# A decoder trunk whose instruction order is planned: 32 plans with wider margins, one of them emitted

## The chip, the cores and the metric

The kernel runs on one core of a Trainium2 chip. A core has five engines that work side by side, each through its own list of instructions in order: TensorE (PE, matrix products; its weight loads are shown apart as PEld), VectorE (DVE), ScalarE (ACT), GpSimd (POOL) and SyncE (SP, which here only issues transfers, DMAs). An engine whose next instruction has to wait holds up all that stands behind it in its list. The metric is the device time of one execution in microseconds (us); lower is better.

## The reference

Two layers of a sequence model over 2048 tokens of width 1024, all in float32. Layer 0 mixes tokens by a gated delta rule (GDN, 8 heads), layer 1 by gated linear attention (GLA, 4 heads). Each has an input projection, a recurrence over chunks of the sequence, a gated RMS norm, an output projection and a layer norm.

```python
def gdn_mixer(x, w_in, conv_w, a_log, dt_bias, norm_w, w_out):
    p = x @ w_in
    qkv = causal_conv_silu(p[..., :GDN_QKV], conv_w)
    ...
    o = gated_delta_rule(q, k, v, g, beta)
    o = gated_rmsnorm(o, norm_w, gate)
    return o.reshape(B, T, GDN_VAL).astype(x.dtype) @ w_out
...
for i in range(DEPTH):
    ...
    x = layer_norm(DEEP_ALPHA * x + y, ln_g[i], ln_b[i])
```

## The kernel before

The work is cut into 48 units: a layer, a group of 512 tokens and a head, in the order of `PHASES` (L1189: GDN groups 0 and 1, GLA group 0, GDN 2, GLA 1, GDN 3, GLA 2, GLA 3). A GDN unit has four parts. `gemms` (L650) multiplies the group's tokens by the head's columns of the input matrix: for each 128 rows of it a chunk `wc` holds a rounded high part and a remainder in two halves, and three 512-column products (high by high, high by low, low by high: `xh,wc`, `xl,wc`, `xh,wc`) go into a `psg` bank of PSUM. `gdn_prep` (L800) builds a triangular matrix and inverts it: 32-wide blocks by a loop of 31 steps on VectorE (`Xt` and `X`, L861 to L866) that reads rows spread to all partitions by eight DMAs (`Arep`, L855), then larger blocks on TensorE with ScalarE copying between the products (`U` to `W2` to `U`, L870 to L885). `gdn_chain` (L1020) runs the recurrence, with a ScalarE copy `wt` between two of its products. `outs` (L1095) multiplies by the output matrix into the one bank of `pso`, six products at a time, and VectorE adds each bank into `y` (L1119) before the next six may start.

Chunks of the input matrix come from memory as `wraw` and are split by ScalarE and GpSimd in the first units (L529); from the third unit on the split chunk is written back (`wk`, L531), and each later group reads it from there straight into `wc` (L516). `wc` has 9 buffers (L1180), so a reload can start only when TensorE has read the chunk that was in the buffer. All these loads, the spread rows `Arep`, the stores `out` and the loads of `y` stand in one list on SP.

No engine's order is written by hand. The unit functions only record operations (`Recorder.note`, L133), with their dependences, a rank (L1185: recurrence before preparation before output before projection), and an estimated time: `cost`, how long the engine is held, and `lag`, how much later the result can be used (L183 to L232). `place` (L234) is a list scheduler: it keeps a clock for each engine, always takes the engine that can go first, gives it the ready operation of the best rank, hands out the buffers as they come free, and so fixes the order. `emit` (L357) then issues the operations in that order, and the hardware's engines go through their lists with real waits. The whole program is issued through one line, L364, so the profile's rows are told apart by the tiles' names.

Of the kernel before, what the change touches and what calls it, by code (L numbers as in the profile page):

```python
# [107 lines left out]

class Op:
    __slots__ = ("key", "call", "name", "args", "kw", "prio", "cost", "lag", "deps", "users", "waits", "ready",  # L110
                 "views", "fresh", "start", "at", "func", "unit")


def size_of(shape):
# [6 lines left out]
class Recorder:  # L121
# [226 lines left out]
    def stuck(self, parked, free, order_of, turn):  # L348
        for tag, ops in parked.items():
# [4 lines left out]
            nxt = {k[1]: ts[turn[k]].at if turn[k] < len(ts) and ts[turn[k]] else None for k, ts in order_of.items() if k[0] == tag}  # L354
            print("   live", live, "next", nxt)

    def emit(self, tc):  # L357
        if INSPECT:
            INSPECT(self)
        def real(a):  # L360
            return a.real() if isinstance(a, View) else a

        for op in self.place():
            tc.keep_in_program_order(op.call(*[real(a) for a in op.args], **{k: real(a) for k, a in op.kw.items()}))  # L364


# [11 lines left out]
LAG, DRAIN = 60, 35  # L378
DMA_LAG, REP_LAG, SLACK = 3500, 7000, 100
INSPECT = None  # L380


@with_exitstack
# [846 lines left out]
```

## Time and profile before

| what | value |
|---|---|
| median of 3 runs | 3030.2 us (3029.43 to 3033.52) |
| the profiled execution, its own time | 3028.51 us |
| its span, first to last instruction | 3026.3 us |
| mean granted TensorE clock over the span | 0.988 |
| TensorE busy / VectorE busy | 2926.2 us / 2201.4 us |
| HBM read and written | 480.36 MB, 129.30 MB |

The profile is a record of one execution. A row of the list of waits names the engine that waited, what it waited for, the sum in us, how often, and the longest. A row of the windows view gives, for a stretch of the span, each engine's busy time, then the granted TensorE clock (1.00 is full speed), the DMA engines' busy share and GB/s. A row of the timeline gives start, length, engine, line, operation, tiles written and read, and in brackets the engine's idle time before it and what ended that. A matmul's shown length holds its passage through the array, and the next starts before it ends, so the distance from start to start is what one costs. A 4-byte product (`f32` on both sides) goes as two instructions.

### The profile page before, as it was taken

How to read it: one execution, taken by the hardware profiler on the slowest of the kernel's cores; microseconds unless marked ns; L12 is line 12 of the kernel's file. 1: busy time of each engine (PE TensorE's matmuls, PEld its weight loads, DVE VectorE, ACT ScalarE, POOL GpSimd, SP SyncE). 2: the span in 40 equal slices, each digit the busy share in tenths (PEclk: the TensorE clock that was granted, in tenths of full speed). 3: DMA queues.
4: the chain of work that ended last, by engine and by line, in shares of the span. 5: the costliest groups of instructions: out<-in, count | busy, mean ns of one | idle time of the engine just before them, and what ended most of it. 6: DMA issues, size and time to landing. Idle time of an engine off the chain costs nothing. (4 is left out here: it accounts for less than half of the span.)

```text
span 3026.3 us, 48052 instructions
## 1 busy us (share of the span) xinstructions
PE 2926.2 (97%) x16172; PEld 2419.0 (80%) x16172; DVE 2201.4 (73%) x5374; ACT 1243.6 (41%) x3233; POOL 499.8 (17%) x848
## 2 busy tenths in 40 slices
PE   8899999999999999999999999999999999999997
PEld 6677777778877887887888888887787888888886
DVE  6878788797777686668778778557787777755655
ACT  5445554543332455333343344333343344433331
POOL 5432444320100233210000000001010000000000
PEclk9999999999999999999999999999999999999998
DMA  6566777695565658687556665768655565857654
GB/s 193 175 196 203 239 234 241 209 293 159 167 182 178 191 165 269 213 286 224 161 163 182 190 207 179 242 228 244 175 171 176 154 193 176 268 192 236 221 183 143
DMA packets 480615, 612.87 MB, mean 203 GB/s; under 512 B 57280, under 2 KB 407744, under 8 KB 464240
## 3 DMA queue, kind: packets, MB, share of 16 engines
q1 hardware_dynamic: 449456, 589.81, 62.9%
q10 hardware_dynamic: 30912, 20.00, 2.4%
q8 instruction: 127, 2.08, 0.3%
q14 instruction: 120, 0.98, 0.1%
HBM read 480.36 MB, written 129.30 MB: 201 GB/s over the span
## 5 line engine op out<-in xcount | busy, mean ns | idle before, releaser
L364 PE MATMUL psg<-xh,wc 128*128 128x512 f32 x3936 | 1349.5, 409 | 29.0 <-DMA wc<-wk 16.3
L364 PEld LDWEIGHTS psg<-xh,wc 128*128 128x128 f32 x3936 | 740.5, 190 | 195.8 <-DMA wc<-wk 20.6
L364 PE MATMUL psg<-xl,wc 128*128 128x512 f32 x1968 | 805.8, 410 | 0.2
L364 PE MATMUL pso<-wo,oth 128*128 128x512 f32 x1472 | 486.1, 406 | 19.1 <-DVE y L364 17.6
L364 PEld LDWEIGHTS psg<-xl,wc 128*128 128x128 f32 x1968 | 374.4, 190 | 76.4 <-DVE xl L364 1.7
L364 DVE SCALAR_TENSOR_TENSOR y<-pso,z,y 128x512 f32<-128x512 f32 x368 | 274.9, 747 | 148.6 <-PE pso L364 127.6
L364 DVE SCALAR_TENSOR_TENSOR acc<-pb,taps,acc 128x512 f32<-128x512 f32 x384 | 300.3, 785 | 76.5 <-ACT acc L364 69.2
L364 POOL TENSOR_TENSOR wc<-wraw,wc 128x256 fp32r<-128x256 f32 (+1 forms) x336 | 283.3, 859 | 423.5 <-ACT wc L364 360.3
L364 PEld LDWEIGHTS pso<-wo,oth 128*128 128x128 f32 x1472 | 263.9, 189 | 82.8 <-DVE y L364 29.0
L364 PE MATMUL pso<-wo,otl 128*128 128x512 f32 x736 | 295.8, 402 | 0.6 <-DVE otl L364 0.6
L364 PE MATMUL psg<-wc,xh 128*128 128x256 f32 (+1 forms) x1344 | 265.3, 289 | 6.2 <-DMA wc<-wk 4.6
L364 DVE TENSOR_TENSOR Xt<-Arep,X 128x124 f32<-128x124 f32 (+30 forms) x992 | 238.6, 241 | 30.6 <-DMA Arep<-blk 7.5
L364 DVE TENSOR_TENSOR X<-X,Xt 128x124 f32<-128x124 f32 (+30 forms) x992 | 242.6, 245 | 23.9
L364 ACT ACTIVATE th<-psg 128x512 f32<-128x512 f32 (+1 forms) x170 | 95.2, 572 | 334.4 <-PE psg L364 315.4
L364 PEld LDWEIGHTS psg<-wc,xh 128*128 128x128 f32 x1344 | 214.6, 189 | 15.0 <-DMA wc<-wk 4.6
L364 PE MATMUL psg<-wc,xl 128*128 128x256 f32 (+1 forms) x672 | 189.4, 287 | 0.0
L364 ACT CAST wc<-wraw 128x256 fp32r<-128x256 f32 (+1 forms) x336 | 126.0, 405 | 116.2 <-DMA wraw<-in_w_in 99.3
L364 PEld LDWEIGHTS pso<-wo,otl 128*128 128x128 f32 x736 | 139.1, 189 | 30.6 <-DVE otl L364 1.6
L364 POOL TENSOR_SCALAR z<-ssq 128x4 f32<-128x4 f32 x44 | 16.8, 383 | 804.7 <-ACT junk L364 804.2
L364 ACT COPY pb<-psg 128x512 f32<-128x512 f32 x128 | 74.8, 585 | 148.4 <-PE psg L364 145.6
L364 POOL COPY halo<-pb 128x3 f32<-128x3 f32 x128 | 35.2, 275 | 577.6 <-ACT pb L364 576.3
L364 PEld LDWEIGHTS psg<-wc,xl 128*128 128x128 f32 x672 | 126.1, 189 | 2.7
(193 smaller groups left out, 4280.3 us busy)
## 6 DMA issues: line engine op xcount, KB each, us to landing
wc<-wk SPq DMA_DIRECT2D x856, 256.0 KB, 3.8
wo<-wok SPq DMA_DIRECT2D x70, 1024.0 KB, 5.0
wk<-wc SPq DMA_DIRECT2D x272, 256.0 KB, 3.0
wraw<-in_w_in SPq DMA_DIRECT2D x336, 128.0 KB, 3.5
Arep<-blk SPq DMA_DIRECT2D x128, 256.0 KB, 5.4
wok<-wo SPq DMA_DIRECT2D x24, 1024.0 KB, 5.3
wc<-wk SPq DMA_DIRECT2D x80, 272.0 KB, 5.3
Arep<-blkq SPq DMA_DIRECT2D x128, 128.0 KB, 6.4
```

What stands on the lines that cost most here:

```text
L364: tc.keep_in_program_order(op.call(*[real(a) for a in op.args], **{k: real(a) for k, a in op.kw.items()}))
```

## The change

`place` is now called by a new function `choose`, 32 times. Each time the costs of all operations are set anew: 20 ns more for each VectorE operation, 300 ns more until a ScalarE result can be used, a transfer's time to landing times 1.3, and every cost times a drawn factor between 0.98 and 1.02. The order that comes out is then carried out by a second model, `carry_out`: engines in order, the plain costs, landing times from a table by tile (`LANDINGS`) times a drawn factor, at most eight transfers under way, and VectorE operations that are now and then 450 ns longer while GpSimd is at work. Four draws are averaged, and the order with the earliest mean end is emitted. The operations, their number, the tiles and the buffers stay the same; the order on every engine changes, and with it which buffer a tile gets.

```diff
+    def choose(self):
+        import random
+        true = [(op.cost, op.lag) for op in self.ops]
+        for op in self.ops:
+            op.real = self.landing(op)
+        best = None
+        for n in range(N_PLANS):
+            draw = random.Random(n)
+            for op, (cost, lag) in zip(self.ops, true):
+                more, times, late = MARGIN.get(op.key, (0, 1.0, 0))
+                op.cost, op.lag = (cost + more) * draw.uniform(0.98, 1.02), lag * times + late
+                op.waits, op.ready = len(op.deps), 0.0
...
+            placed = self.place()
...
+            rows = self.plan(placed)
+            ends = sum(self.carry_out(rows, random.Random(100 + k)) for k in range(N_DRAWS)) / N_DRAWS
+            if best is None or ends < best[0]:
+                best = ends, placed, [(t, t.slot) for op in placed for t in op.fresh]
+        for t, slot in best[2]:
+            t.slot = slot
+        self.expected = best[0]
+        return best[1]
+
+    def landing(self, op):
+        if op.name != "dma_start":
+            return op.cost, op.lag
+        tag = op.args[0].of.tag.split("_")[0] if isinstance(op.args[0], View) else "out"
+        return LANDINGS.get(tag, (430, 3500))
+
+    def plan(self, placed):
...
+            deps = [(at[d], 0 if order else 1 if d.key == op.key == "v" else 3 if op.key == "t" else 2)
+                    for d, order in op.deps.items()]
+            rows.append(("s" if op.key == "a" else op.key, *op.real, deps, frees, op.func, op.name == "dma_start"))
+        return rows
+
+    def carry_out(self, rows, draw):
+        clock, landed, beside = dict.fromkeys("vsgtd", 0.0), [], []
...
+            if dma:
+                if len(landed) >= 8:
+                    now = max(now, landed[-8])
+                lag *= draw.lognormvariate(0, 0.15)
...
+            elif e == "v":
+                beside = [b for b in beside if b[1] > now]
+                if any(b[0] < now + cost for b in beside) and draw.random() < 0.3:
+                    cost += 450
+            elif e == "g":
+                cost *= draw.uniform(1.0, 1.3)
+                beside.append((now, now + cost))
+            clock[e] = now + cost
...
+        return max(seen)
...
-        for op in self.place():
+        for op in self.choose():
...
+N_PLANS, N_DRAWS = 32, 4
+MARGIN = {"v": (20, 1.0, 0), "s": (0, 1.0, 300), "a": (0, 1.0, 300), "d": (0, 1.3, 0)}
+LANDINGS = {"xraw": (450, 5000), "wraw": (465, 3500), "y": (430, 6500), "woraw": (430, 4300), "gcT": (326, 3560),
...
+            "wk": (519, 3040), "wo": (326, 5000), "wc": (518, 3970), "x2": (540, 3860), "x2T": (326, 4530),
```

What it does to the order is seen at two places. The first is SP's list at the first head of the last GDN group (the 25th of 32 groups of `Arep` loads, at 2077 to 2100 us of the span before): reloads of chunks (`wc` from `wk`) for the next head, the eight spread loads `Arep` of this head, and stores of the finished group (`out` from `y`). Before:

```order
L364 DMA wc_141<-wk_0_453 128x2x256
L364 DMA wc_142<-wk_0_454 128x2x256
L364 DMA wc_143<-wk_0_455 128x2x256
L364 DMA Arep_206<-blk_4914_0_607 32x2048 x4
L364 DMA Arep_206<-blkq_4915_0_608 32x1024 x4
L364 DMA wc_139<-wk_0_456 128x2x256
L364 DMA wc_144<-wk_0_457 128x2x256
L364 DMA wc_145<-wk_0_458 128x2x256
L364 DMA wc_137<-wk_0_459 128x2x256
L364 DMA wc_140<-wk_0_460 128x2x256
```

The same place in SP's list now:

```order
L456 DMA wc_143<-wk_0_455 128x2x256
L456 DMA wc_142<-wk_0_456 128x2x256
L456 DMA wc_144<-wk_0_457 128x2x256
L456 DMA wc_145<-wk_0_458 128x2x256
L456 DMA wc_137<-wk_0_459 128x2x256
L456 DMA wc_138<-wk_0_460 128x2x256
L456 DMA Arep_206<-blk_4914_0_607 32x2048 x4
L456 DMA Arep_206<-blkq_4915_0_608 32x1024 x4
L456 DMA wc_139<-wk_0_461 128x2x256
L456 DMA out<-y_223 128x512
```

The chunks `wk_0_456` to `wk_0_460` moved from behind the eight spread loads to ahead of them.

The second place is TensorE's list in the preparation of the seventh unit (GDN group 0, head 6; 413 to 421 us before), where ScalarE copies the result of the products `psc<-U,D` into `W`, which the products `psc<-W,Tm` read. Around them stand products of the projection (`psg`) and of the output (`pso`). Before:

```order
L364 MATMUL psc_169<-U_201,D_0_179 32x32 x8
L364 MATMUL pso_232<-wo_228,oth_213 128x512
L364 MATMUL pso_232<-wo_228,otl_215 128x512
L364 MATMUL psg_109<-xh_125,wc_137 128x512
L364 MATMUL psc_167<-W_0_202,Tm_200 32x32 x8
L364 MATMUL psg_111<-xh_122,wc_143 128x512
L364 MATMUL psg_111<-xl_130,wc_143 128x512
L364 MATMUL psg_111<-xh_122,wc_143 128x512
L364 MATMUL psg_109<-xh_126,wc_138 128x512
L364 MATMUL psc_169<-U_201,D_0_179 64x64 x4
```

The same step in TensorE's list now:

```order
L456 MATMUL psc_169<-U_201,D_0_179 32x32 x8
L456 MATMUL pso_232<-wo_228,oth_214 128x512 x2
L456 MATMUL pso_232<-wo_228,otl_216 128x512
L456 MATMUL pso_232<-wo_228,oth_213 128x512 x2
L456 MATMUL psc_167<-kq_116 128x256
L456 MATMUL psc_169<-W_0_202,Tm_200 32x32 x8
L456 MATMUL psc_167<-kq_116 128x256
L456 MATMUL pso_232<-wo_228,otl_215 128x512
L456 MATMUL psg_110<-xh_125,wc_137 128x512
L456 MATMUL psg_110<-xh_126,wc_138 128x512
L456 MATMUL psg_110<-xl_134,wc_138 128x512
L456 MATMUL psc_169<-U_201,D_0_179 64x64 x4
```

Between `U,D` and `W,Tm` stood three 512-column products and now stand five and one of 256 columns in 4-byte form; between `W,Tm` and the next `U,D` stood four and now stand four and one of 256 columns.

More of the change, by code (lines that the diff above doesn't have):

```diff
@@ L110 @@
     __slots__ = ("key", "call", "name", "args", "kw", "prio", "cost", "lag", "deps", "users", "waits", "ready",
-                 "views", "fresh", "start", "at", "func", "unit")
+                 "views", "fresh", "start", "at", "func", "unit", "real")
 def size_of(shape):
@@ L355, in stuck @@
             print("   live", live, "next", nxt)
+    def choose(self):
[10 more added lines that the diff above has]
+                op.waits, op.ready = len(op.deps), 0.0
+                for t in op.views:
+                    t.left, t.seen, t.slot = 0, [], None
+            for op in self.ops:
+                for t in op.views:
+                    t.left += 1
+            placed = self.place()
+            for op, (cost, lag) in zip(self.ops, true):
+                op.cost, op.lag = cost, lag
+            rows = self.plan(placed)
[6 more added lines that the diff above has]
+        return best[1]
@@ new lines, in landing @@
+    def landing(self, op):
[4 more added lines that the diff above has]
+    def plan(self, placed):
+        at = {op: i for i, op in enumerate(placed)}
+        users, last, rows = {}, {}, []
+        for i, op in enumerate(placed):
+            for t in op.views:
+                users.setdefault(t, []).append(i)
+        for i, op in enumerate(placed):
+            frees = set()
+            for t in op.fresh:
+                if (t.tag, t.slot) in last:
+                    frees.update(users[last[t.tag, t.slot]])
+                last[t.tag, t.slot] = t
+            deps = [(at[d], 0 if order else 1 if d.key == op.key == "v" else 3 if op.key == "t" else 2)
+                    for d, order in op.deps.items()]
+            rows.append(("s" if op.key == "a" else op.key, *op.real, deps, frees, op.func, op.name == "dma_start"))
+        return rows
@@ new lines, in carry_out @@
+    def carry_out(self, rows, draw):
+        clock, landed, beside = dict.fromkeys("vsgtd", 0.0), [], []
+        table = {"t": False, "s": None}
+        done, seen = [], []
+        for e, cost, lag, deps, frees, func, dma in rows:
+            now = clock[e]
+            for d, how in deps:
+                now = max(now, done[d] if how == 0 else done[d] + rows[d][2] - LAG + DRAIN if how == 1 else
+                          seen[d] + (100 if how == 3 else 0))
+            for d in frees:
+                now = max(now, done[d] if rows[d][0] == e and not rows[d][6] else seen[d])
+            if dma:
+                if len(landed) >= 8:
+                    now = max(now, landed[-8])
+                lag *= draw.lognormvariate(0, 0.15)
+            elif e == "t":
+                cost += 2.3
+                if func != table[e]:
+                    table[e], cost = func, cost + (110 if func else 190)
+            elif e == "s" and func is not None and func != table[e]:
+                table[e], cost = func, cost + 1280
+            elif e == "v":
[6 more added lines that the diff above has]
+            clock[e] = now + cost
+            done.append(now + cost)
+            seen.append(now + cost + lag)
+            if dma:
+                landed.append(seen[-1])
+        return max(seen)
@@ L380 @@
 INSPECT = None
+N_PLANS, N_DRAWS = 32, 4
+MARGIN = {"v": (20, 1.0, 0), "s": (0, 1.0, 300), "a": (0, 1.0, 300), "d": (0, 1.3, 0)}
+LANDINGS = {"xraw": (450, 5000), "wraw": (465, 3500), "y": (430, 6500), "woraw": (430, 4300), "gcT": (326, 3560),
+            "Gb": (326, 3690), "wok": (335, 5250), "blk": (326, 1757), "blkq": (545, 2730), "Arep": (418, 6000),
+            "wk": (519, 3040), "wo": (326, 5000), "wc": (518, 3970), "x2": (540, 3860), "x2T": (326, 4530),
+            "out": (412, 4600), "xh": (445, 6600), "xl": (383, 7000), "oth": (445, 6600), "otl": (383, 7000)}
 @with_exitstack
```

## The prediction

> **What bounds the kernel now.** I read the page's busy times first, then TensorE by stage, then whom TensorE waits for, then the places of the longest waits in the timeline with the clock beside them.
>
> ```profile
> PE 2926.2 (97%) x16172; PEld 2419.0 (80%) x16172; DVE 2201.4 (73%) x5374; ACT 1243.6 (41%) x3233; POOL 499.8 (17%) x848
> ```
>
> TensorE is the bound: of the span of 3026.3 us it is idle for 3026.3 - 2926.2 = 100.1 us. The number of products does not change, so only this idle time, and time in which the clock is low, can go. By stage (windows: span, PE busy, PEld, DVE, ACT, POOL, then the clock):
>
> ```profile
> 0.00:700.00 700.00, 651.44 (x3355) 512.29 (x3356) 558.21 (x1349) 344.98 (x961) 263.29 (x390) 0.99 0.73 220
> 2040.00:2130.00 90.00, 81.35 (x359) 65.11 (x358) 68.65 (x178) 28.46 (x79) 12.04 (x28) 0.96 0.80 244
> 2130.00:2800.00 670.00, 668.96 (x3829) 562.71 (x3828) 479.84 (x1204) 260.37 (x653) 46.22 (x106) 1.00 0.63 193
> 3006.00:3026.30 20.30, 4.95 (x21) 3.36 (x19) 16.60 (x28) 0.00 (x0) 3.30 (x6) 0.76 0.28 104
> ```
>
> Of the 100.1 us, 48.6 lie in the first 700 us, where GpSimd still splits chunks; 8.7 in 90 us around 2080; 15.4 in the tail, where VectorE ends alone; only 1.0 in 2130 to 2800. TensorE's own waits, whole run (sum, times, longest), the eight largest:
>
> ```profile
> PE psg L364 <- DMA wc<-wk: 20.9, 14, 4.6
> PE pso L364 <- DVE y L364: 17.6, 18, 2.8
> PE psg L364 <- DVE acc L364: 4.5, 6, 1.4
> PE psg L364 <- ACT wc L364: 4.0, 5, 1.9
> PE psg L364 <- ACT acc L364: 3.9, 4, 2.1
> PE psc L364 <- DVE og L364: 3.7, 3, 2.6
> PE psh L364 <- DVE S L364: 2.7, 4, 1.5
> PE psc L364 <- ACT oth L364: 2.6, 3, 1.3
> ```
>
> Reloaded chunks are the largest item, then the one `pso` bank waiting for VectorE.
>
> **Part 1: reloads.** The longest waits of all, in the timeline (start, length, then idle time before):
>
> ```profile
> 955.78 0.80 PE L364 MATMUL psg<-xh,wc 128*128 128x512 f32 x1 [2.94 <-DMA wc<-wk]
> ```
>
> ```profile
> 1372.04 0.39 PE L364 MATMUL psg<-xl,wc 128*128 128x512 f32 x1
> 1372.27 0.39 PE L364 MATMUL psg<-xh,wc 128*128 128x512 f32 x1
> 1375.70 0.80 PE L364 MATMUL psg<-xh,wc 128*128 128x512 f32 x1 [3.05 <-DMA wc<-wk]
> 1376.30 0.63 PE L364 MATMUL psg<-xl,wc 128*128 128x512 f32 x1
> 1376.72 1.05 PE L364 MATMUL psg<-xh,wc 128*128 128x512 f32 x2
> ```
>
> ```profile
> 2099.64 0.80 PE L364 MATMUL psg<-xh,wc 128*128 128x512 f32 x1 [4.61 <-DMA wc<-wk]
> ```
>
> A 512-column product costs 0.23 us from start to start (1372.04 to 1372.27), and 0.42 just after the wait (1376.30 to 1376.72): the clock fell. So a long wait costs twice. The windows at the low clock, and the wait before one of them:
>
> ```profile
> 456.40:458.60 2.20, 0.00 (x0) 0.00 (x0) 2.03 (x8) 0.00 (x0) 0.00 (x0) 1.00 0.87 213
> 460.10:463.50 3.40, 3.40 (x9) 2.65 (x9) 3.12 (x11) 0.41 (x1) 0.92 (x3) 0.50 1.04 338
> 955.00:961.90 6.90, 6.12 (x15) 4.79 (x15) 3.30 (x10) 0.60 (x1) 0.00 (x0) 0.51 0.65 216
> 1374.80:1381.70 6.90, 6.00 (x16) 4.86 (x17) 1.19 (x5) 1.52 (x7) 0.00 (x0) 0.51 0.64 198
> 2098.50:2105.30 6.80, 5.13 (x13) 3.73 (x14) 1.02 (x4) 0.09 (x1) 0.00 (x0) 0.50 0.66 209
> ```
>
> Half of the busy time at half clock is lost: 3.1 us at 955, 3.0 at 1375, 2.6 at 2099. With the waits: 6.0, 6.1 and 7.2 us.
>
> A 2.2 us wait was enough at 456. [...]
>
> Why were these chunks late? SP's list before 2099:
>
> ```profile
> 2084.65 1.89 SPq L364 DMA_DIRECT2D wc<-wk  x3
> 2086.64 1.94 SPq L364 DMA_DIRECT2D Arep<-blk  x4
> 2088.62 3.89 SPq L364 DMA_DIRECT2D Arep<-blkq  x4
> 2093.50 6.93 SPq L364 DMA_DIRECT2D wc<-wk  x4
> ```
>
> The list of transfers has the median time from issue to landing in its last column:
>
> ```profile
> wc<-wk SPq DMA_DIRECT2D x856, 256.0 KB, 3.8
> ```
>
> The eight spread loads hold SP for 1.94 + 3.89 = 5.8 us, and the chunk behind them lands 3.8 us (median) after its issue: about 10 us, with its own 0.5. In the order, 36 products stand between TensorE's last read of its buffer and the first use of the new chunk: 36 x 0.23 = 8.3 us. It must be late. In the new order this chunk and four more stand ahead of the spread loads. It has 28 products, 6.4 us, against 0.6 + 3.8, and the first chunk behind the spread loads has 45 and four transposes, over 10 us. I take the 7.2 us as gone. At 955 it is the same: the late chunk stood right behind a head's spread loads with 32 products, 7.4 us, and now stands ahead of them: 6.0 gone. At 1375 the late chunk had 39 products; in the new order one chunk fewer stands ahead of the spread loads, and the first behind them has 39 again: no cure, and I take a quarter of 6.1, 1.5. The other eleven reload waits make 20.9 - 4.6 - 2.9 - 3.1 = 10.3 us; a landing planned 1.3 times as long issues loads earlier, and I take half, 5.1. Together 7.2 + 6.0 + 1.5 + 5.1 = **19.8 us less**. The bounds: all of it, 29.6; or half of the first two, nothing at 1375 and five us of new waits, 1.6 less.
>
> Who pays: the spread loads of that head go out five issues, 5 x 0.63 = 3.2 us, later, and wait for TensorE to free those five buffers. Behind them waits VectorE's loop of `Xt` and `X`. In 2098.5 to 2105.3 VectorE is busy for 1.02 of 6.80 us, so it has room to catch up, and `U`, the loop's result, is not among TensorE's eight largest waits: under 2.6 us for all 32 preparations. Cost nothing; with the cover gone, 3.2 us a unit.
>
> **Part 2: ScalarE, 300 ns.** The second place of the order:
>
> ```profile
> 414.93 0.71 PE L364 MATMUL psc<-W,Tm 32*32 32x32 f32 x16 [0.56 <-ACT W L364]
> ...
> 418.04 0.68 PE L364 MATMUL psc<-U,D 128*64 128x64 f32 x8 [1.04 <-ACT U L364]
> ```
>
> Two products and one 4-byte one more stand between (about 0.7 us), so the 0.56 goes and the 1.04 is shortened by about 0.2. Over all 96 such copies, the median work between rises from three products to five. The rows for ScalarE's `wc`, `acc` and `oth` with these two are 5 + 4 + 3 + 2 = 14 waits; 0.3 us of each, 4.2 us, and a little for those under a weight load: **5 us less**. Bounds: 12 less (all of it); 5 more, if ScalarE's other work is put ahead.
>
> **Part 3: VectorE, 20 ns.** Nearly all of the `pso` waits fall into the first 700 us, where GpSimd is busy for 263 of 700 us (46 of 670 in 2130 to 2800); first the row of waits of that stage, then VectorE there:
>
> ```profile
> PE pso L364 <- DVE y L364: 17.1, 16, 2.8
> ```
>
> ```profile
> 454.38 0.69 DVE L364 TENSOR_TENSOR X<-X,Xt 128x100 f32<-128x100 f32 x1
> 455.10 0.68 DVE L364 TENSOR_TENSOR Xt<-Arep,X 128x96 f32<-128x96 f32 x1
> 455.82 0.68 DVE L364 TENSOR_TENSOR X<-X,Xt 128x96 f32<-128x96 f32 x1
> 456.54 0.25 DVE L364 TENSOR_TENSOR Xt<-Arep,X 128x92 f32<-128x92 f32 x1
> ...
> 457.85 0.74 DVE L364 SCALAR_TENSOR_TENSOR y<-pso,z,y 128x512 f32<-128x512 f32 x1
> ```
>
> The same kind of step takes 0.68 or 0.25 us. Three long ones put VectorE 3 x 0.43 = 1.3 us behind the plan, and `y` is queued behind them while TensorE stands before `pso` (the 2.2 us without a product from 456.40 above). Ten steps give the plan 0.2 us of margin: it dulls this and does not remove it. 18 waits x 0.2 = 3.6 us, with a little of the clock: **4 us less**. Bounds: 17.6 less (all `pso` waits gone), 14 more (the four VectorE rows above, 17.6 + 4.5 + 3.7 + 2.7 = 28.5, half as much again).
>
> **Part 4: what the margins cost.** Planned lateness also makes gaps: where nothing else is ready, TensorE's next product is put behind one that waits. 1349 VectorE steps of the first 700 us times 20 ns are 27 us. Nothing of it costs if other products fill in, as in 2130 to 2800 (VectorE 480 of 670 us, 1.0 us idle); all of it where none do. VectorE's share in the first stage, 558 of 700, is not much above, so nearer the low end: **4 us more**, bounds 0 and 27. The tail has the same sequence of rows in both orders, two banks exchanged: 0.
>
> **The sum**: -19.8 - 5 - 4 + 4 = -24.8 us, against this execution's own 3028.5 (span 3026.3 and 2.2 around it): 3003.7. The median of the runs is 1.7 us above the profiled time: about **3005**.
>
> **The rivals.** *More goes than I count*: VectorE's waits too, because the drawn delays are chosen against. All favourable bounds: 29.6 + 12 + 17.6 = 59 us, less the 4: near 2975. For it: the waits are few and long. Against it: the delays come at random times, and the plan is fixed.
>
> *The gain is given back*: 32 candidates differ by 2 per cent in the costs and are judged by a model; if real lateness comes from what it has not got, the pick is no better than the order before. Old waits go, others of like size appear: about 3028. For it: only the reload waits can be read off the order as cured.
>
> *Slower: the margin turns into planned idle time.* Its place is the first 700 us, where VectorE is busy for 80% (558 of 700) and 1349 steps hold 27 us of margin. If TensorE's order there follows VectorE's late plan, products stand behind results that the plan expects late, and the 27 us become idle, with the clock falling at some of the gaps as at 456. With the unsure halves of parts 1 to 3 missing as well, the gain is the 13 us of the two cured places: 3030 + 27 - 13 = 3044. It decides once more than half of the margin, 13 us, becomes idle. Against it: VectorE at 72% (480 of 670) leaves TensorE 1.0 us idle in 2130 to 2800, so other products fill in.
>
> **How the numbers follow.** The forecast (2985 to 3020) 0.55; more (2960 to 2985) 0.15; given back (3020 to 3036) 0.17; slower (above) 0.13. A measurement of this kernel tells about 0.2%, 6 us, from no change. Faster than 3024: 0.55 + 0.15 and a quarter of the third, 0.74; within, 0.13; slower 0.13. The range leaves out most of the slower case and the far end of the better one: 2968 to 3034.
>
> **What would show it.** Right: the reload row falls from 20.9 to near 10 us with no wait near 4 us, no half clock at the place of 2099 or 955, the copies `W` and `U` nearly gone from TensorE's waits, `pso` near 14. Wrong: `pso`, `acc` or `U` rows grown by over 10 us, TensorE idle over 60 us in the first 700, or new waits for chunks behind other loads.

## The result and the profile after

| kernel | median | range | runs |
|---|---|---|---|
| before | 3029.81 us | 3027.96 to 3033.52 | 4 |
| after | 3012.15 us | 3008.54 to 3015.85 | 4 |

The ratio is 0.9945, with a 95% interval of 0.9929 to 0.9961: 0.0055 x 3030 = 16.7 us less. The profiled execution of after took 3008.54 us (span 3006.4, mean clock 0.996), that of before 3028.51 (3026.3, 0.988). After's is the fastest of its four runs, and the clock of the other three was 0.993 to 0.995, so its trace flatters the change a little. First the row of busy times on the page of after:

```profile
PE 2909.3 (97%) x16172; PEld 2405.1 (80%) x16172; DVE 2204.9 (73%) x5374; ACT 1242.9 (41%) x3233; POOL 497.2 (17%) x848
```

Of the 19.9 us that the span lost, TensorE's busy time gave 2926.2 - 2909.3 = 16.9 and its idle time 100.1 - 97.1 = 3.0. The number of products is the same, so the busy time fell with the clock, 0.996 against 0.988 over the span. The windows of after (span, PE, PEld, DVE, ACT, POOL, clock) show where:

```profile
0.00:700.00 700.00, 650.98 (x3375) 511.92 (x3376) 566.50 (x1350) 343.08 (x961) 262.95 (x390) 1.00 0.73 220
700.00:1000.00 300.00, 300.00 (x1604) 245.99 (x1603) 224.15 (x614) 115.50 (x313) 23.67 (x64) 1.00 0.61 177
...
2040.00:2130.00 90.00, 81.49 (x391) 63.58 (x390) 63.79 (x159) 33.57 (x89) 9.46 (x29) 0.98 0.82 247
2130.00:2800.00 670.00, 664.76 (x3796) 558.90 (x3795) 479.59 (x1203) 257.57 (x645) 41.03 (x98) 1.00 0.62 190
```

The place of 955 is cured: TensorE is idle for nothing from 700 to 1000. The 90 us around 2080 are as idle as before (8.5 against 8.7), the first 700 us too (49.0 against 48.6), and 2130 to 2800 has 4.2 us more of idle time. TensorE's waits, whole run (sum, times, longest):

```profile
PE psg L456 <- DMA wc<-wk: 15.3, 13, 2.9
PE pso L456 <- DVE y L456: 12.7, 17, 1.8
PE psg L456 <- ACT wc L456: 7.0, 9, 1.7
PE psg L456 <- DVE acc L456: 5.8, 8, 1.1
PE psc L456 <- DVE kd L456: 3.6, 2, 2.2
PE psg L456 <- DVE xl L456: 3.1, 4, 2.0
PE pso L456 <- DVE otl L456: 3.0, 7, 0.7
```

The reload row fell from 20.9 to 15.3 and `pso` from 17.6 to 12.7; ScalarE's `wc` rose from 4.0 to 7.0, and the rows of VectorE's `kd`, `xl` and `otl`, 1.4 us, nothing and 0.6 before, have 3.0 to 3.6. What changed is how long the single wait is: before had 11 waits of over 2 us, after has 5. And with them went the half clock. The trace's record of the granted clock has, before the tail, 13 stretches at half clock before (61.4 us together) and 3 in after (10.2 us). All three of after, in windows:

```profile
45.00:48.50 3.50, 3.19 (x12) 2.48 (x13) 1.36 (x6) 0.91 (x4) 0.00 (x0) 0.65 0.94 362
212.90:216.30 3.40, 3.08 (x7) 2.42 (x8) 3.26 (x9) 0.90 (x3) 3.32 (x5) 0.56 0.85 262
2097.50:2100.90 3.40, 3.19 (x9) 2.53 (x10) 0.00 (x0) 0.00 (x0) 0.00 (x0) 0.50 0.87 311
```

Half of TensorE's busy time inside such stretches, the tail's with them, is 28.3 us before and 5.0 in after. These 23.3 us are more than the 16.9 by which the busy time fell; the other 6.4 us went the other way, and where was not followed.

The third stretch stands near the place whose cure the prediction counted on. TensorE there, in the timeline of after:

```profile
2088.96 0.50 PE L456 MATMUL psg<-xh,wc 128*128 128x512 f32 x1 [2.71 <-DMA wc<-wk]
2089.29 0.40 PE L456 MATMUL psg<-xl,wc 128*128 128x512 f32 x1
...
2097.71 0.80 PE L456 MATMUL psg<-xh,wc 128*128 128x512 f32 x1 [2.92 <-DMA wc<-wk]
2098.30 0.63 PE L456 MATMUL psg<-xl,wc 128*128 128x512 f32 x1
```

SP's list in the same stretch:

```profile
2064.56 5.39 SPq L456 DMA_DIRECT2D wc<-wk  x8
2070.00 2.60 SPq L456 DMA_DIRECT2D Arep<-blk  x4
2073.03 8.83 SPq L456 DMA_DIRECT2D Arep<-blkq  x4
2081.96 0.52 SPq L456 DMA_DIRECT2D wc<-wk  x1
2082.58 1.02 SPq L456 DMA_DIRECT2D out<-y  x2
2083.69 1.19 SPq L456 DMA_DIRECT2D wc<-wk  x2
...
2088.93 3.32 SPq L456 DMA_DIRECT2D y<-in_x  x2
2093.66 2.50 SPq L456 DMA_DIRECT2D wc<-wk  x3
```

The longest wait of SP itself inside this block of spread loads, and the one of before at its place:

```profile
SPq L456 <- DMA Gb<-gcT: 5.5, 1, 5.5
```

```profile
SPq L364 <- DMA Gb<-gcT: 4.5, 1, 4.5
```

The chunks that now stand ahead of the spread loads left in time, and so did the first one behind them. But the eight spread loads held SP for 2.60 + 8.83 = 11.4 us instead of 5.8: the last of them waited 5.5 us until an earlier transfer, ScalarE's `Gb`, had landed. Before had a like wait of 4.5 us just behind the spread loads and the chunk after them. The first of the two chunks issued from 2083.69 on came 2.71 us late, less than SP had lost there. So the wait of 4.61 us became one of 2.71, for a later chunk. The other wait, of 2.92, is not new: it is for the chunk behind the loads of `y`, and before had the same one, after which its clock did not fall:

```profile
2120.09 0.50 PE L364 MATMUL psg<-xh,wc 128*128 128x512 f32 x1 [2.69 <-DMA wc<-wk]
```

The half clock of after at 2097.5 stands at this old wait.

### The profile page after: what moved, and what is told of

Read it like the earlier page. It is cut to its first block, busy times and chain, and to the rows that moved or that the text cites. A ratio compares the mean times of both kernels' runs of the same rounds, so it can differ in the third digit from the quotient of the medians.

```text
span 3006.4 us, 48053 instructions
## 1 busy us (share of the span) xinstructions
PE 2909.3 (97%) x16172; PEld 2405.1 (80%) x16172; DVE 2204.9 (73%) x5374; ACT 1242.9 (41%) x3233; POOL 497.2 (17%) x848
## 5 line engine op out<-in xcount | busy, mean ns | idle before, releaser
L456 PEld LDWEIGHTS psg<-xh,wc 128*128 128x128 f32 x3936 | 733.1, 189 | 188.2 <-DMA wc<-wk 17.0
L456 PE MATMUL psg<-xl,wc 128*128 128x512 f32 x1968 | 796.1, 405 | 0.8 <-DVE xl L456 0.7
L456 PE MATMUL pso<-wo,oth 128*128 128x512 f32 x1472 | 492.5, 407 | 13.9 <-DVE y L456 12.7
L456 DVE TENSOR_TENSOR Xt<-Arep,X 128x124 f32<-128x124 f32 (+30 forms) x992 | 243.1, 245 | 31.4 <-DMA Arep<-blk 10.2
L456 PEld LDWEIGHTS psg<-wc,xh 128*128 128x128 f32 x1344 | 212.1, 188 | 18.4 <-DMA wc<-wk 3.7
```

## Experiments

Three theories were open. **A, the margins** make the gain, by issuing loads earlier (the prediction's Part 1). **B, the choice** makes it: the model finds, among drawn plans, one in which TensorE waits in shorter pieces. **C, the draw** makes it: plans differ by chance, and the model tells little. And beside them, whether the clock is the cause or only goes along with it.

**Margins alone.** One plan, no draw, no choice:

```diff
-        for n in range(N_PLANS):
+        for n in PLANS:
-                op.cost, op.lag = (cost + more) * draw.uniform(0.98, 1.02), lag * times + late
+                op.cost, op.lag = cost + more, lag * times + late
-N_PLANS, N_DRAWS = 32, 4
+PLANS, N_DRAWS = (0,), 1
```

> One plan alone, with the margins, without drawn costs and without a choice among plans. If the margins make the gain, it comes to 3007 to 3020 us, with TensorE's clock at 0.993 or higher and at most five half-clock stretches. If the choice among 32 makes it, this one stays at 3024 to 3036 us. In both, the sum of TensorE's idle time stays between 90 and 110 us if it is the clock and not the waits that separates the orders; if shorter waits were the cause, a faster run here has visibly less idle time (under 85 us).

Measured: 3021.4 us, ratio 0.9984 (0.9973 to 0.9996), 5 us of the 17: between the two expected ranges. The idle time, 97.4 us, is not less. Its profiled execution was the fastest of its twelve, and its clock of 0.995 stands against a mean of 0.992 over the twelve, so the 17.1 us of half clock in its trace are, by estimate, fewer than in its median run.

**Choice alone.** The 32 draws without margins; the plan that the model puts first is draw 19:

```diff
-N_PLANS, N_DRAWS = 32, 4
-MARGIN = {"v": (20, 1.0, 0), "s": (0, 1.0, 300), "a": (0, 1.0, 300), "d": (0, 1.3, 0)}
+PLANS, N_DRAWS = (19,), 1
+MARGIN = {}
```

> No margins: the plan that the choice among 32 takes when only the costs are drawn by 2 per cent. If the choice makes the gain, 3008 to 3020 us; if the margins do, 3022 to 3036 us with chunks behind the spread loads late again (waits for reloads near 20 us, longest 3 us or more) and a clock near 0.988.

Measured: 0.9956 (0.9941 to 0.9972), 0.0044 x 3025 = 13 us less. Its two largest rows of TensorE's waits:

```profile
PE psg L456 <- DMA wc<-wk: 22.8, 15, 4.8
PE pso L456 <- DVE y L456: 13.8, 19, 2.2
```

The row of reloads has not fallen (20.9 before; the wait at 955 is gone here too, a wait of 4.8 us near 2085 is not), and the kernel is nearly as fast as after. That speaks against A.

**The last of the 32.** Margins and draws as in the change, but the plan that the model puts last (draw 22: `PLANS, N_DRAWS = (22,), 1`).

> With the margins and the drawn costs, but the plan that the second model puts last of the 32 instead of first. If that model judges well, this is clearly slower than the emitted plan: 3028 to 3045 us. If the 32 are alike on the chip and the margins do all, 3008 to 3020 us.

Measured: 3023.3 us, 0.9992 (0.998 to 1.0004): no gain that the interval tells from none, again between the two expected ranges, with 10 stretches of half clock (44.4 us) in its trace. By itself this fits B and C.

**Margin of the transfers alone.** One plan, `MARGIN = {"d": (0, 1.3, 0)}`, no draw.

> One plan, no draws and no choice, with the margin of the transfers alone (landings planned 1.3 times as long), which Part 1 of the prediction priced at 19.8 us less. Theory (the choice makes the gain, the margins by themselves little): within 0.3% of before, 3018 to 3034. Rival (Part 1 as predicted): 15 to 20 us less than before, ratio near 0.994, the row of waits for reloaded chunks from 20.9 to near 10.

Measured: 0.9999 (0.9986 to 1.0011). Here the wait at 955 is gone, at the place of 2099 a later chunk behind the spread loads waits 2.89 us instead of the 4.61 (at 2110, with nothing over 0.51 from 2075 to 2105), the reload row fell to 15.9, almost as far as in after, and the time stayed. Its four largest rows of waits:

```profile
PE psg L456 <- DMA wc<-wk: 15.9, 12, 4.1
PE pso L456 <- DVE y L456: 11.9, 18, 1.8
PE psg L456 <- ACT wc L456: 7.4, 4, 6.1
PE psc L456 <- DVE U L456: 5.8, 4, 2.3
```

New long waits took their place, the longest of them behind other loads, in its timeline:

```profile
1184.52 10.84 SPq L456 DMA_DIRECT2D wraw<-in_w_in  x7
...
1193.79 2.06 ACT L456 CAST wc<-wraw 128x256 fp32r<-128x256 f32 x6 [0.51 <-DMA wraw<-in_w_in]
...
1194.24 0.80 PE L456 MATMUL psg<-xh,wc 128*128 128x512 f32 x1 [6.10 <-ACT wc L456]
```

Seven loads of a first-time chunk take SP 10.84 us, ScalarE splits the chunk when it has landed, and TensorE has waited 6.10 us. This is the rival "given back", shown for a single plan.

**Filling the waits of before.** Is the clock a cause? 57 more 512-column products, whose results nobody reads, write into the `pso` bank. They stand ahead of eight products at which TensorE waited long, none of them a `pso` product, so that it is busy there and waits less:

```diff
-        for op in self.place():
+        ones, xh, d = (self.tags[k][0][:] for k in ("ones", "xh", "pso"))
+        for i, op in enumerate(self.place()):
+            for _ in range(FILL.get(i, 0)):
+                tc.keep_in_program_order(tc.nc.tensor.matmul(d, ones, xh, start=True, stop=True))
+FILL = {385: 6, 608: 6, 722: 3, 728: 4, 786: 4, 11708: 10, 17648: 16, 17790: 8}
```

> The order of before, with 57 more 512-column products whose results nobody reads, put ahead of eight products that wait long (three for reloads at 1375, 2099 and 2120 us, five in the first 100 us); they are shorter than the waits that they fill. If the clock falls because TensorE stands idle, the half-clock stretches near 88, 98, 1375 and 2098 us go, and the run is 6 to 10 us faster than before although it does 13 us more work (3020 to 3024 us, clock 0.991 to 0.993). If the low clock costs nothing beside the waits, or comes from something else, the time stays within 3 us of before or grows by up to 5 us.

Measured: 0.9989 (0.9979 to 0.9999). Of the four half-clock stretches aimed at, three were gone from the trace (near 88, 1375 and 2098 us); others stood elsewhere (11 in all, 41.0 us). Idle time fell by 10.8 us to 89.3, and busy time rose by 4.9 us for 57 x 0.23 = 13 us of added products. That fits the theory of the clock, but 3 us of effect lie between the two expectations and are too small to settle it.

**The price of a wait by its length.** So it was measured by itself, with the same waiting in few or in many pieces. In the kernel before, ahead of the first product of chosen `pso` banks between 704 and 2985 us, a 128-column product goes into the bank and ScalarE copies out of it; the bank's next product has to wait for the copies. `zz` is a new tile that nobody reads.

```diff
-        for op in self.place():
+        ones, xh, d, z = (self.tags[k][0][:] for k in ("ones", "xh", "pso", "zz"))
+        for i, op in enumerate(self.place()):
+            if i in HOLD:
+                tc.keep_in_program_order(tc.nc.tensor.matmul(d[:, :128], ones, xh[:, :128], start=True, stop=True))
+                for _ in range(COPIES):
+                    tc.keep_in_program_order(tc.nc.scalar.copy(z, d[:, :256]))
+COPIES = 7
```

> The kernel before with 28 long waits put into TensorE's list between 704 and 2985 us, ahead of the first product of a pso bank: one 128-column product into the bank, then seven ScalarE copies of 256 columns out of it (0.37 us each by the trace of before), for which the bank's next product has to wait. About 28 x 2.9 = 81 us of waits in all, 2 us of products. Theory (the length of a wait decides how often the clock falls): of the waits of 2.5 to 3 us in the six traces so far 16 of 22 were followed by a half clock within 3.5 us, so some 20 more stretches of 3.41 us, each costing 1.7: TensorE's busy time 2926 + 2 + 35 = near 2963, the whole near 3030 + 81 + 37 = 3148. Rival (only the sum of idle time counts): busy time and clock as in the run with short waits, within 8 us of it for the same sum of idle time.

With `COPIES = 2` and 84 places:

> The same with 84 waits of two copies each, near 1.0 us: the same 84 us in all, and 6 us of products, in three times as many pieces. Theory: of the waits of 0.5 to 1.5 us in the six traces 22 of 257 were followed by a half clock, so some 7 more stretches of 1.7 us: busy time 2926 + 6 + 12 = near 2944, the whole near 3030 + 84 + 18 = 3132; mean clock clearly above that of the run with long waits. Rival (only the sum of idle time counts): as many half-clock stretches per microsecond of idle time as in the run with long waits.

Measured: 1.0415 (1.0391 to 1.044) with long waits, 3155.59 us, and 1.0312 (1.0288 to 1.0337) with short ones, 3122.79 us; before stood at 3030.09 beside them. The busy times of TensorE came out at 2963.1 and 2944.6 us, where 2963 and 2944 were expected. The second agreement is luck: 7 half-clock stretches more than before were expected, and there were 4 fewer. The products put in (6 us) and the slower first product after each wait (an estimated 84 x 0.1 = 8 us, by the starts given in the last section) are a part of what made up for it; the rest was not followed. The run with long waits, its row of waits and one of its places in the timeline:

```profile
PE pso L369 <- ACT zz L368: 83.6, 28, 4.3
```

```profile
1841.30 0.73 PE L369 MATMUL pso<-wo,oth 128*128 128x512 f32 x2 [2.89 <-ACT zz L368]
```

The windows of the same run around that place, and its body after 700 us:

```profile
1838.90:1842.00 3.10, 0.70 (x3) 0.61 (x4) 0.79 (x4) 2.19 (x6) 0.00 (x0) 1.00 0.33 120
1842.50:1845.90 3.40, 3.40 (x13) 3.06 (x13) 2.30 (x10) 0.00 (x0) 0.00 (x0) 0.50 0.01 2
1845.90:1849.30 3.40, 3.40 (x25) 3.21 (x24) 2.06 (x10) 0.00 (x0) 0.00 (x0) 0.99 0.60 157
...
700.00:3124.00 2424.00, 2306.44 (x12833) 1929.89 (x12832) 1627.13 (x4000) 972.69 (x2470) 232.57 (x452) 0.98 0.61 189
```

The run with short waits, its row of waits and its body:

```profile
PE pso L369 <- ACT zz L368: 73.5, 84, 0.9
```

```profile
700.00:3096.40 2396.40, 2290.11 (x12893) 1909.43 (x12892) 1630.61 (x4000) 960.41 (x2445) 233.45 (x452) 1.00 0.62 191
```

The run with 28 waits of about 3 us has 26 stretches of half clock before its tail (122.9 us; before 13 and 61.4), that with 84 waits of under 1 us has 9 (37.5 us). In the part where the waits were put in, from 704 us on, these are 20 stretches (102.4 us) with long waits, 5 (17.1 us) with short ones and 6 (34.1 us) in before. During or within 3.5 us after an inserted wait a half clock began at 16 of the 28 long ones and at 1 of the 84 short ones. The mean clock of the four runs is 0.977 with long waits and 0.990 with short ones, as in before. A microsecond of waiting cost 125.5 / 83.6 = 1.50 us in long pieces and 92.7 / 73.5 = 1.26 in short ones (the products put in are a part of the latter). That only the sum of idle time counts is refuted: it matters how the idle time is cut up.

**The change again, and more plans.** The last runs ask whether the model's list is worth anything (B against C). Each is the changed kernel with one plan: `PLANS, N_DRAWS = (12,), 1` for the second, 3 for the third, 14 for the seventeenth, and 94 for the first of 160 draws.

> The changed kernel again, beside the margin of the transfers alone. Both theories: 0.9945 of before, as in its first comparison; half-clock stretches in the run fewer than 7.

> The plan with margins that the model puts second of the 32 (draw 12; the changed kernel emits draw 9). Theory (the model finds plans in which TensorE waits in shorter pieces): near the first, ratio 0.993 to 0.997, under 8 half-clock stretches. Rival (the model tells little, draw 9 is a lucky one): anywhere among the unselected plans with margins, ratio 0.997 to 1.001, 8 to 13 stretches.

> The plan that the model puts third (draw 3). The same two expectations: 0.993 to 0.997 by the theory, 0.997 to 1.001 by the rival. If one of the second and third is near the first and the other is not, the model helps and luck does too.

> A plan from the middle of the model's list (draw 14, the 17th of the 32). Theory: between the first and the last, ratio 0.996 to 0.999. Rival: the same spread as for every other plan with margins.

> The plan that the model puts first of 160 draws (draw 94), which it takes to be a little earlier than draw 9, by much less than draw 9 stands ahead of the middle. Theory: 0.993 to 0.996, within what the measurement tells from the changed kernel. Rival: 0.997 to 1.001.

The table has all plans of this study in which nothing is put in. The ratio and the clock (a mean over runs) come from all runs; the other columns from the one profiled execution: TensorE's idle time, its waits of over 2 us, and half-clock stretches before the tail.

| plan | ratio, 95% | clock | idle us | over 2 us | half clock |
|---|---|---|---|---|---|
| before (69 runs) | 1 | 0.990 | 100.1 | 11 | 13, 61.4 us |
| after: 1st of 32 | 0.9945 (0.9929 to 0.9961) | 0.995 | 97.1 | 5 | 3, 10.2 us |
| after again | 0.9942 (0.992 to 0.9964) | 0.995 | 94.0 | 4 | 6, 23.9 us |
| 2nd of 32 | 0.9952 (0.9939 to 0.9965) | 0.993 | 98.4 | 5 | 6, 23.9 us |
| 1st of 32 without margins | 0.9956 (0.9941 to 0.9972) | 0.993 | 97.2 | 7 | 7, 30.7 us |
| 17th of 32 | 0.9959 (0.9945 to 0.9974) | 0.992 | 96.3 | 6 | 10, 37.5 us |
| 1st of 160 | 0.9977 (0.9968 to 0.9987) | 0.993 | 101.6 | 8 | 6, 30.7 us |
| margins, no draw | 0.9984 (0.9973 to 0.9996) | 0.992 | 97.4 | 10 | 5, 17.1 us |
| 3rd of 32 | 0.9991 (0.9982 to 1.0001) | 0.991 | 103.6 | 12 | 10, 37.5 us |
| 32nd of 32 | 0.9992 (0.998 to 1.0004) | 0.992 | 102.2 | 9 | 10, 44.4 us |
| margin of transfers, no draw | 0.9999 (0.9986 to 1.0011) | 0.991 | 106.9 | 7 | 11, 44.4 us |

The second plan came out as B expected; the third did not; the middle one is as fast as the second; the first of 160, which the model takes to be the earliest of all, came out in the rival's range. So the model's list does not order these plans, and B falls as far as that. What goes with the time is the number of waits of over 2 us: 4 to 7 in the five fast rows, 7 to 12 in the others. The sum of idle time goes with it nearly as well (94.0 to 98.4 us against 97.4 to 106.9), so this table by itself does not part the two; the inserted waits do. Whether a pick by this model is better than a blind draw stays open: the three plans that it puts first of a set have 0.9945, 0.9956 and 0.9977, four others with draws have 0.9952, 0.9959, 0.9991 and 0.9992, and that is too few to tell. None of the plans is shown to beat after. And none of the nine other orders is slower than before. So before may itself be a slow draw, and part of the gain no more than leaving it; no run here tests that.

## Why the prediction was right, and where not

It said 3005 us, range 2968 to 3034, and faster as the likeliest: 3012 was measured. Sign and range are right. The mechanism, long waits that cost twice, is right too; where the gain would come from was not, and that the sum came so near is in part luck: every plan of the table lies in that range, and the margin of the transfers, priced at 19.8 of the 24.8 us, gave nothing by itself (0.9999).

**The sum.** Its -24.8 us were 18.4 of waits and 6.4 of clock (2.6 at 2099, 3.1 at 955, a quarter of 3.0 at 1375). The profiled pair measured 3.0 of waits and 16.9 of busy time. The step that failed is "I take the 7.2 us as gone", and its likes in parts 1 to 3: each wait was priced as if nothing took its place. Most came back as shorter ones, 97.1 us of idle time against 100.1, and what was gained is mainly that they are shorter. Over all runs the mean clock rose from 0.990 to 0.995, which at 3027 us is 0.0047 / 0.990 x 3027 = 14 of the 16 us between the means.

**Part 1, reloads (-19.8).** The row fell by 5.6, not by 13.4. At 955 the reasoning held, and 6.0 us went. At 2099 the counts held for the chunks ahead of the spread loads and for the first one behind them; what failed is that the spread loads would hold SP for 5.8 us in the new order too. They held it for 11.4, with SP's wait for `Gb` now among them, and the wait moved to a later chunk, 2.71 us for 4.61. The sum also had nothing for the wait that before had at 2120, 2.69 us without a half clock: in after it is 2.92 us with one. That a smaller row of reloads brings no time by itself is shown by the margin of the transfers alone: 15.9 us, ratio 0.9999, since other waits took its place.

**Part 2, ScalarE (-5).** The rows for `W` and `U` are gone, as predicted. But `wc` took back 3.0 us: ScalarE's waits together did not fall. Net nothing.

**Part 3, VectorE (-4).** `pso` fell by 4.9, near 14 as the forecast wanted; other VectorE rows (`kd`, `xl`, `otl`) took it back.

**Part 4 (+4).** Idle time of the first 700 us rose by 0.4, and the rival "planned idle time" did not come: its sign would have been over 60 us there, and 49.0 were measured. 2130 to 2800 has 4.2 us more of idle time, the size of the term at another place; that the margins made it is not shown.

**Given back** was the rival that described the waits best; it missed that waits of a like sum in shorter pieces cost less.

**The clock.** The prediction used one row, the 2.2 us wait at 456. With twelve traces (all but the two with waits put in) there is a curve. TensorE's waits by length, and during or within 3.5 us after how many of them a half clock began:

| length, us | waits | with a half clock | share |
|---|---|---|---|
| 0.5 to 1 | 333 | 26 | 0.08 |
| 1 to 1.5 | 174 | 15 | 0.09 |
| 1.5 to 2 | 77 | 16 | 0.21 |
| 2 to 2.5 | 38 | 21 | 0.55 |
| 2.5 to 3 | 35 | 28 | 0.80 |
| over 3 | 19 | 16 | 0.84 |

In these rows no single length parts the waits with a half clock from those without: the share goes from 0.09 at 1 to 1.5 us over 0.21 and 0.55 to 0.80 at 2.5 to 3, and a half clock came with 49 of 73 waits of 2 to 3 us. In the twelve traces TensorE was idle for 1.3 to 3.4 of the 3.41 us ahead of every stretch, and every stretch of half clock inside the runs lasts 3.41 us or a multiple.

The traces say more. In each of them, by its record of the granted clock, all half-clock stretches start whole multiples of 3.413 us apart: in before at 16.36, 88.04, 98.28 and 207.51 us, that is 21, 3 and 32 of them. Cut at these points, the twelve traces have 10443 windows at full clock. Of 10179 in which TensorE was idle for under 1.2 us in all, none was followed by a half clock; of 193 with 1.2 to 2.0 us, 39 were; of 71 with more, all. So in these traces the half clock went with the idle time inside one such window, the sum of its shorter waits too: ahead of the stretches of before at 88.04 and 98.28 TensorE was idle for 2.25 and 2.16 us, with no single wait over 1.4. How a long wait lies to these points shows at two places: the 2.69 us ahead of 2120.09 in before have such a point inside them, at 2118.97, which leaves 1.57 us in one window and 1.12 in the next, and no half clock followed; of the 2.92 us ahead of 2097.71 in after, 2.69 lie in one window, and a half clock began at its end, 2097.48. No run here put several short waits into one window on purpose.

What is not settled: the clock does not explain every plan. The row "17th of 32" is fast with a clock of 0.992, that of "margins, no draw"; its idle time is 1.1 us less, and where the rest of their 0.25% lies was not followed.

## What to carry to other kernels

Before counting a cured wait as gain, ask what waits next on the same engine: here TensorE was idle for 97 us instead of 100 after margins had been put against its longest waits, and a wait of 4.6 us came back as one of 2.7 for a later chunk. A wait of TensorE of over 2 us costs its length and most often a stretch at half clock (65 of 92 here), while the same waiting in pieces of under 1 us costs its length and a little (1.26 us for each microsecond, with the products put in); so break up long waits first, keep the pieces apart, and count idle time by windows (here of 3.41 us), not only by sum. When a scheduler's small random changes move the time by 0.5% and its own model does not order them, a gain from "choosing" is first of all the gain of one draw: measure several picks before crediting the rule that picked.

## What the runs showed of the hardware that was not expected

- One kernel varies with its clock from run to run: 69 runs of before lie between 3016.5 and 3038.6 us with mean clocks from 0.993 to 0.987, and time and clock go together (correlation -0.77; what else varies was not followed). A single profiled execution need not have the clock of the other runs: that of "margins, no draw" has a mean clock of 0.995, its twelve runs 0.992.
- The first product after a wait costs more at full clock as well: 2088.96 to 2089.29 in the timeline of after is 0.33 us to the next start, against 0.23 in a full stream. In before it is 0.33 to 0.35 us for all 22 such pairs of 512-column products after a wait of over 0.5 us, in after for all 26. Over 84 waits that is an estimated 8 us, a part of why the short waits cost 1.26 us for each microsecond.
